# A state-space layer's output gathered for two chunks at a time: one TensorE burst and one PSUM bank in place of two

## The chip, the cores and the metric

The kernel runs on one core of one Trainium2 chip. The metric is the device time of one execution in microseconds; several runs are made and their median is taken. One execution is recorded by the hardware profiler. The engines are TensorE (PE, with its weight loads shown apart as PEld), VectorE (DVE), ScalarE (ACT), GpSimd (POOL) and SyncE (SP), which here only issues DMAs. Each engine takes its own instructions strictly in the order in which they stand in the program; engines wait for each other through semaphores.

## What is computed

The reference is an encoder of two layers over 1024 tokens of width 1024. Layer 0 is attention and is not touched. Layer 1 is a bidirectional state-space (Mamba-2 SSD) layer, with 32 heads in 8 groups of 4, 128 states and chunks of 128 tokens. Cut to what matters (one direction):

```
xbc = silu(conv(h @ w_in))            # x, B, C; z and dt come from the same product
cb = einsum('bclgn,bcsgn->bcgls', cc, bc)
y_diag = einsum('bcgrls,bclgrp...', cb * decay, x * dt)
states = einsum('bclgn,bclgrp->bcgrpn', bc, x * dt * decay_states)
carry = carry * chunk_decay + states  # over the chunks, one after the other
y_off = einsum('bclgn,bcgrpn->bclgrp', cc, carry_before) * exp(acs)
y = (y_diag + y_off of both directions + x * d_skip) * silu(z)
```

After it come an RMS norm, the product with `w_out`, a gate, a residual and a last norm. Everything is float32; the large products are made exact enough by splitting each operand into a rounded high part and a low rest (three matmuls for one).

## The kernel before, in words

**Two streams in one.** The SSD work of a group of heads is too small to fill TensorE, so it is laid between the large matmuls of the projection `w_in` for the next group. `group_dense(g)` gives the dense stream: six blocks per group, in the order x0, z0, x1, B, C, z1. One block has 48 matmuls of 128x512 (L359 to L361, "dense" from here on) and fills two of the four PSUM banks named `acc`; the block after the next takes the same two banks again. A block of x0, x1, B or C is read from its banks eight times by VectorE, the taps of the convolution (L1336, in the rows `big<-acc,cv,big`), after ScalarE has put the middle tap into SBUF (L1328). The weights are loaded by SP, rounded by ScalarE (`whi`, L254), and the rest is made by VectorE (`wlo`, L255).

`ssd_items(g)` gives the other stream: a list of items, each with the time that it is thought to take on PE and DVE. `balance` lays the two streams into one order by these numbers. So a changed number or a merged item moves dense matmuls and SSD items against each other on all engines.

**The items of a group**, with the lines that the text speaks of:

- `A1(c)` turns x and B of chunk c by PE transposes (L1412). `A2(j)` scales x (`xd`, L1424), makes the chunk's states on PE (L1425) and adds the decayed carry: a product into a tile `sw` (L1434) and a sum into the new carry `SS` (L1435).
- `B0(c)` loads the summed decays of chunk c into a tile `acs` (one DMA of 512 KB issued by SP).
- `B1(c)`, for c from 7 down to 0: VectorE makes `E` (L1449, four instructions), PE the product of B and C (L1452), VectorE masks it into `cb` (L1455), ScalarE takes exponentials (`E`, L1457), copies `cb` times dt into `W` (L1459) and exponentials of `acs` (L1461).
- `M(c)`: VectorE adds the other direction to `W` (L1471, four), multiplies `E` by `W` (L1473) and `acs` by C (L1476).
- `B2(c)`: PE gathers y of chunk c in one bank (L1487; 12 matmuls with 64 columns of weights, 8 for the first and last chunk; the trace has two records for each), VectorE adds the skip term into `yt` (L1491, two of 128x128), GpSimd multiplies z by it (L1495, two of 128x128). It comes after `M` of the chunk below, right behind the product of `B1(c-2)`.

The y banks are `a2` and `a3` in turn. The buffers: `sw` 1, `acs` 4, `E` 3, `W` 2, `yt` 2 (128x256 each).

In group 7 the dense stream is the first part of the output product (L1004 to L1006), which asks of VectorE one scaled rest (L1584) and one `wlo` for every 12 matmuls.

Of the kernel before, what the change touches and what calls it, by code (L numbers as in the profile page):

```python
# [11 lines left out]
F32 = mybir.dt.float32  # L12
# [3 lines left out]
OP = mybir.AluOpType  # L16

P = 128
# [73 lines left out]
class Trunk:  # L92
# [1302 lines left out]
    def ssd_items(self, g):  # L1395
        nc = self.nc
        st = self.grp[g]
        ident = self.c("ident")
        C = 8
        hs = slice(4 * g, 4 * g + 4)  # L1400
        xt, bt, SS, live = {}, {}, {}, {}

        def ck(c):
            return slice(P * c, P * c + P)

        def coef(t, c):
            return t[:, c].rearrange("p (d h) -> p d h", d=2)[:, :, hs, None].to_broadcast([P, 2, 4, 64])

        def A1(c):
            p = self.bank("a0", [P, 3, P], 2)  # L1410
            for i, n in enumerate(("x0", "x1", "B")):
                nc.tensor.transpose(p[:, i], st[n][:, ck(c)], ident)  # L1412
            x = xt[c] = self.u("xt", [P, 4, 64], F32, 8)
            nc.scalar.copy(x.rearrange("p h q -> p (h q)"), p[:, :2].rearrange("p i q -> p (i q)"))
            b = bt[c] = self.u("bt", [P, P], F32, 8)
            nc.scalar.copy(b, p[:, 2])

        def A2(j):

            if j < C - 1:  # L1420
                p = live["s", j] = self.bank("a3" if j % 2 else "a2", [P, 2, 4, 64])
                for d, c in enumerate((j, C - 1 - j)):
                    xd = self.u("xd", [P, 4, 64], F32, 3)
                    nc.vector.tensor_mul(xd, xt[c], coef(self.dtdec, c)[:, d])  # L1424
                    nc.tensor.matmul(p[:, d].rearrange("p h q -> p (h q)"), bt[c], xd.rearrange("p h q -> p (h q)"),  # L1425
                                     start=True, stop=True)
            if j:
                p = live.pop(("s", j - 1))
                s = SS[j - 1] = self.u("SS", [P, 2, 4, 64], F32, 7)
                if j == 1:  # L1430
                    nc.scalar.copy(s, p)
                else:
                    w = self.u("sw", [P, 2, 4, 64])
                    nc.vector.tensor_mul(w, SS[j - 2], coef(self.cdec, j - 1))  # L1434
                    nc.vector.tensor_add(s, p, w)  # L1435

        def B0(c):
            a = live["a", c] = self.u("acs", [P, 2, 4, P], F32, 4)
            nc.sync.dma_start(a, self.acsd[c, :, hs][None].to_broadcast([P, 2, 4, P]))

        def dirs(c):

            return [d for d, k in ((0, c > 0), (1, c < C - 1)) if k]

        def B1(c):
            a = live["a", c]
            E, W = live["G", c] = self.u("E", [P, 4, P], F32, 3), self.u("W", [P, 4, P], F32, 2)
            for h in range(4):
                nc.vector.scalar_tensor_tensor(E[:, h], a[:, 0, h], self.delta[:, c, 4 * g + h:4 * g + h + 1], a[:, 1, h],  # L1449
                                               op0=OP.add, op1=OP.min)  # L1450
            p = self.bank("a0", [P, P], 2)
            nc.tensor.matmul(p, st["B"][:, ck(c)], st["C"][:, ck(c)], start=True, stop=True)  # L1452
            cb = live["cb", c] = self.u("cb", [P, 2, P])
            tri = self.cst[:, CST["upper"][0]:CST["lower"][1]].rearrange("p (d l) -> p d l", d=2)
            nc.vector.tensor_mul(cb, p[:, None].to_broadcast([P, 2, P]), tri)  # L1455
            for h in range(4):
                nc.scalar.activation(E[:, h], E[:, h], AF.Exp, bias=self.nacb[:, c, 4 * g + h:4 * g + h + 1])  # L1457
            for h in range(4):
                nc.scalar.activation(W[:, h], cb[:, 0], AF.Copy, scale=self.dt[:, c, 4 * g + h:4 * g + h + 1])  # L1459
            ds = slice(dirs(c)[0], dirs(c)[-1] + 1)  # L1460
            nc.scalar.activation(a[:, ds], a[:, ds], AF.Exp)  # L1461
            if c == 0 and g < 7:
                nc.scalar.preload_act_table_set(SILU)

        def M(c):

            cb = live.pop(("cb", c))
            E, W = live["G", c]
            for h in range(4):
                hh = 32 + 4 * g + h  # L1470
                nc.vector.scalar_tensor_tensor(W[:, h], cb[:, 1], self.dt[:, c, hh:hh + 1], W[:, h],  # L1471
                                               op0=OP.mult, op1=OP.add)
            nc.vector.tensor_mul(E, E, W)  # L1473
            ds = dirs(c)
            a = live["a", c][:, ds[0]:ds[-1] + 1].rearrange("p d h l -> p (d h) l")
            nc.vector.tensor_mul(a, a, st["C"][:, None, ck(c)].to_broadcast([P, 4 * len(ds), P]))  # L1476

        def B2(c):

            y = self.bank("a3" if c % 2 else "a2", [P, 2, P])  # L1480
            G, _ = live.pop(("G", c))
            ea = live.pop(("a", c))
            for r in range(2):
                mms = [(SS[6 - c if d else c - 1][:, d], ea[:, d]) for d in dirs(c)] + [(xt[c], G)]
                for k, (w, m) in enumerate(mms):
                    for i in range(2):
                        nc.tensor.matmul(y[64 * i:64 * i + 64, r], w[:, 2 * r + i], m[:, 2 * r + i],  # L1487
                                         start=k == 0, stop=k == len(mms) - 1)
            t = self.u("yt", [P, 2, P], F32, 2)
            for r in range(2):  # L1490
                nc.vector.scalar_tensor_tensor(t[:, r], st[f"x{r}"][:, ck(c)], self.sv[:, 2 * g + r:2 * g + r + 1],  # L1491
                                               y[:, r], op0=OP.mult, op1=OP.add)
            for r in range(2):
                z = st[f"z{r}"][:, ck(c)]
                nc.gpsimd.tensor_mul(z, z, t[:, r])  # L1495
            if c == 0 and g == 7:
                self.ylast = [st["z0"], st["z1"]]
            elif c == 0:
                for r in range(2):
                    nc.gpsimd.dma_start(self.yd[2 * g + r], st[f"z{r}"])  # L1500

        def a1(c):
            return 200, lambda: A1(c), 0.35, 0.8

        def a2(j):
            return 900, lambda: A2(j), 0.9, 2.3

        items = []
        for j in range(C // 2):
            items += [a1(j), a1(C - 1 - j)]  # L1510
            if j:
                items.append(a2(j - 1))
        items.append((1, lambda: (B0(C - 1), B0(C - 2)), 0, 0))
        items += [a2(j) for j in range(C // 2 - 1, C)]
        if g == 7:
            items.append((1500, lambda: None, 0, 2.0))
        for c in range(C - 1, -1, -1):
            items.append((900, lambda c=c: B1(c), 0.25, 1.6))
            if c < C - 2:
                items.append((500, lambda c=c: B2(c + 2), 1.7, 0.6))  # L1520
            items.append((1150, lambda c=c: M(c), 0, 3.0))
            if c > 1:
                items.append((1, lambda c=c: B0(c - 2), 0, 0))
        items += [(500, lambda: B2(1), 1.7, 0.6), (900, lambda: None, 0, 1.5), (500, lambda: B2(0), 1.7, 0.6)]
        return items

    def out1(self, tail):
# [301 lines left out]
```

## Time and profile before

| | us |
|---|---|
| median of 3 runs | 1833.21 (1831.17 to 1834.16) |
| the profiled execution, its device time | 1831.87 |
| its span in the trace | 1830.0 |
| SSD stages of groups 0 to 6, from the trace | about 988 to 1590 |
| SSD stage of group 7 | about 1590 to 1671 |

The profile's page gives PE busy for 97% of the span, DVE for 76%, ACT for 53% and POOL for 15%. In the 40 slices of the page DVE stands at 9 tenths through the SSD stages, at 6 or 7 before them. To read it: the share of the span tells which engine could be the limit, and the waits inside one stage tell whether it is. The trace of groups 1 to 6 repeats almost to the hundredth of a microsecond, every 89.3 us, so one group stands for six.

### The profile page before, as it was taken

To read this page: it belongs to the slowest core of one execution; us is meant where nothing else is said; L and a number is where in the kernel's file an instruction comes from. 1 tells how busy PE (TensorE), PEld (TensorE's weight loads), DVE (VectorE), ACT (ScalarE), POOL (GpSimd) and SP (SyncE) were. 2 spreads that over 40 slices of the span, in tenths; PEclk is the share of its full clock that TensorE was granted. 3 is DMA by queue.
4 is the path that set the end of the run, shared out by engine and by line. 5 is a ranking of instruction groups with operands and counts; after the bars stand their busy time and mean duration, and the time that the engine had idled before them with its cause. 6 is when DMAs were issued, how large, how long until landed. Compare 5 with 4: busy or idle time off the path is not lost.

```text
span 1830.0 us, 28629 instructions
## 1 busy us (share of the span) xinstructions
PE 1778.0 (97%) x10136; PEld 1463.5 (80%) x10136; DVE 1395.2 (76%) x3212; ACT 961.9 (53%) x2107; POOL 283.2 (15%) x466
## 2 busy tenths in 40 slices
PE   8999999999999999999999999999999999997997
PEld 6888888878788888789878788888888888776787
DVE  7576667767654664666687989899898989898965
ACT  6655444544454554444444656565656565765532
POOL 3102122112211221010010101010101010114310
PEclk8999999999999999999999999999999999999999
DMA  8132234323311221264213242333333232354542
GB/s 323 55 118 88 94 100 132 96 88 99 90 58 47 79 66 45 78 218 152 82 50 95 71 118 83 111 89 97 97 89 104 82 110 76 116 162 128 190 163 97
DMA packets 99734, 193.66 MB, mean 106 GB/s; under 512 B 15624, under 2 KB 23048, under 8 KB 99592
## 3 DMA queue, kind: packets, MB, share of 16 engines
q1 hardware_dynamic: 86600, 167.32, 29.7%
q0 software_dynamic: 12288, 23.86, 4.7%
q8 instruction: 80, 1.31, 0.3%
q10 hardware_dynamic: 704, 0.66, 0.1%
q14 instruction: 62, 0.51, 0.1%
HBM read 169.00 MB, written 16.48 MB: 101 GB/s over the span
## 4 chain that ended last, share of the span: by engine, by line
PE 83%; DVE 10%; ACT 4%; issue 2%; DMA 1%; SPq 0%; ACTq 0%; DVEq 0%; POOL 0%
PE acc L359 17%; PE acc L361 16%; PE acc L360 16%; PE a L1487 4%; PE a L1425 3%; PE a L1004 3%; PE a L1005 3%; PE a L1006 3%; PE acc L1006 2%; PE a L702 2%; PE acc L1004 2%; PE acc L1005 2%; PE a L687 2%; DVE big L1336 1%; DVE wlo L255 1%
## 5 line engine op out<-in xcount | busy, mean ns | idle before, releaser
L359 PE MATMUL acc<-big,whi 128*128 128x512 f32 (+1 forms) x1520 | 628.0, 413 | 0.8 <-DVE big L1336 0.7
L361 PE MATMUL acc<-big,wlo 128*128 128x512 f32 (+1 forms) x1520 | 593.8, 391 | 0.0
L360 PE MATMUL acc<-big,whi 128*128 128x512 f32 (+1 forms) x1520 | 592.7, 390 | 0.6 <-DVE big L277 0.6
L359 PEld LDWEIGHTS acc<-big,whi 128*128 128x128 f32 x1520 | 287.1, 189 | 66.0 <-issue 15.5
L361 PEld LDWEIGHTS acc<-big,wlo 128*128 128x128 f32 x1520 | 286.4, 188 | 63.1
L360 PEld LDWEIGHTS acc<-big,whi 128*128 128x128 f32 x1520 | 287.8, 189 | 48.4 <-DVE big L277 1.2
L255 DVE TENSOR_TENSOR wlo<-wraw,whi 128x512 fp32r<-128x512 f32 (+1 forms) x297 | 213.5, 724 | 79.8 <-ACT whi L254 76.8
L254 ACT CAST whi<-wraw 128x512 fp32r<-128x512 f32 (+1 forms) x302 | 181.9, 612 | 88.8 <-issue 26.6
L678 ACT ACTIVATE sm<-sm,nb 128x256 f32<-128x256 f32 (+1 forms) x192 | 89.3, 466 | 194.3 <-DVE nb L676 191.6
L1336 DVE SCALAR_TENSOR_TENSOR big<-acc,cv,big 128x512 f32<-128x512 f32 (+1 forms) x248 | 169.3, 741 | 6.5 <-ACT big L1328 6.5
L1495 POOL TENSOR_TENSOR big<-big,yt 128x128 f32<-128x128 f32 x128 | 61.6, 502 | 633.7 <-DVE yt L1491 633.7
L1457 ACT ACTIVATE E<-E,nacb 128x128 f32<-128x128 f32 x256 | 81.8, 391 | 128.7 <-DVE E L1449 113.3
L689 DVE COPY pt<-a 128x512 f32<-128x512 f32 (+1 forms) x96 | 57.6, 600 | 72.8 <-PE a L687 72.8
L673 DVE CUSTOM_DVE_ANT_0 sm<-a,cst 128x256 f32<-128x256 f32 (+1 forms) x192 | 64.9, 375 | 57.7 <-PE a L668 57.4
L1004 PE MATMUL a<-big,whi 128*128 128x256 f32 (+1 forms) x304 | 99.2, 326 | 0.0
L1006 PE MATMUL a<-big,wlo 128*128 128x256 f32 (+1 forms) x304 | 98.0, 323 | 0.7 <-DVE wlo L255 0.7
L1005 PE MATMUL a<-big,whi 128*128 128x256 f32 (+1 forms) x304 | 97.9, 322 | 0.0
L1328 ACT ACTIVATE big<-acc,cv 128x512 f32<-128x512 f32 x62 | 44.5, 770 | 95.2 <-PE acc L361 82.8
L1004 PE MATMUL acc<-big,whi 128*128 128x512 f32 x224 | 91.2, 407 | 2.6 <-ACT big L1348 2.6
L575 POOL DMA_DIRECT2D rt<-kT x92 | 50.3, 559 | 280.3 <-ACT kT L515 185.3
L1005 PE MATMUL acc<-big,whi 128*128 128x512 f32 x224 | 88.4, 395 | 3.1 <-DVE big L255 2.7
L1471 DVE SCALAR_TENSOR_TENSOR W<-cb,dt,W 128x128 f32<-128x128 f32 x256 | 85.1, 388 | 8.1 <-ACT W L1459 6.1
(257 smaller groups left out, 3147.6 us busy)
## 6 DMA issues: line engine op xcount, KB each, us to landing
wraw<-in_win SPq DMA_DIRECT2D x186, 256.0 KB
acs<-acsd SPq DMA_DIRECT2D x64, 512.0 KB
wraw<-in_wout SPq DMA_DIRECT2D x112, 256.0 KB
big<-in_modw SPq DMA_DIRECT2D x48, 512.0 KB
yd<-big POOLq DMA_DIRECT2D x14, 512.0 KB, 4.8
big<-yd SPq DMA_DIRECT2D x28, 256.0 KB
vT<-mix POOLq DMA_DIRECT2D x20, 256.0 KB, 4.9
big<-in_xT SPq DMA_DIRECT2D x8, 512.0 KB
```

Source lines behind the costliest of these rows:

```text
L254: self.nc.scalar.copy(dst_hi, src)
L255: self.late.append((lambda: self.lo_engine.tensor_sub(dst_lo, src, dst_hi.bitcast(F32)), tile))
L359: mm(o, hi[:, cols], x_[:, t0:t0 + n], start=first, stop=False, **kw)
L360: mm(o, hi[:, cols], x_[:, H2 + t0:H2 + t0 + n], start=False, stop=False, **kw)
L361: mm(o, lo[:, cols], x_[:, t0:t0 + n], start=False, stop=last, **kw)
L678: nc.scalar.activation(sm[:, h, :W], sm[:, h, :W], AF.Exp, bias=nb[:, h:h + 1], scale=0.125, accum_out=stat[:, h, 1, i:i + 1])
L1004: mm(o, hi[:, c], x[:, t:t + n], start=kt == 0 and (n == H2 or m % 2 == 0), stop=False, **kw)
L1005: mm(o, hi[:, c], x[:, H2 + t:H2 + t + n], start=False, stop=False, **kw)
L1006: mm(o, lo[:, c], x[:, t:t + n], start=False, stop=kt == nkt - 1, **kw)
L1336: nc.vector.scalar_tensor_tensor(y[:, lo:hi], a[:, lo + o:hi + o], w[:, cv, k:k + 1], y[:, lo:hi], op0=OP.mult, op1=OP.add)
L1457: nc.scalar.activation(E[:, h], E[:, h], AF.Exp, bias=self.nacb[:, c, 4 * g + h:4 * g + h + 1])
L1471: nc.vector.scalar_tensor_tensor(W[:, h], cb[:, 1], self.dt[:, c, hh:hh + 1], W[:, h], op0=OP.mult, op1=OP.add)
```

## The change

The items `B2(c)` of two chunks become one, `B2(c0)` for c0 = 6, 4, 2, 0: the matmuls of chunk c0+1 and then of c0 go into one bank (`a3` for 6 and 2, `a2` for 4 and 0), then two instructions of 128x256 on VectorE and two of 128x256 on GpSimd. The item comes after `B1(c0-2)`; the last two chunks come together at the end. The number of thought times for an item becomes 3.2 and 0.85 (it was 1.7 and 0.6 for one chunk). The decayed carry is made in the tile of the new carry, so `sw` goes. The buffers: `acs` 5, `E` 4, `W` 1, `yt` 1 (128x512). In the changed file the lines after L1434 stand one lower or one higher; the rows of order below have its numbers.

```diff
-                    w = self.u("sw", [P, 2, 4, 64])
-                    nc.vector.tensor_mul(w, SS[j - 2], coef(self.cdec, j - 1))
-                    nc.vector.tensor_add(s, p, w)
+                    nc.vector.tensor_mul(s, SS[j - 2], coef(self.cdec, j - 1))
+                    nc.vector.tensor_add(s, p, s)
...
-            a = live["a", c] = self.u("acs", [P, 2, 4, P], F32, 4)
+            a = live["a", c] = self.u("acs", [P, 2, 4, P], F32, 5)
...
-            E, W = live["G", c] = self.u("E", [P, 4, P], F32, 3), self.u("W", [P, 4, P], F32, 2)
+            E, W = live["G", c] = self.u("E", [P, 4, P], F32, 4), self.u("W", [P, 4, P])
...
-        def B2(c):
+        def B2(c0):
-            y = self.bank("a3" if c % 2 else "a2", [P, 2, P])
-            G, _ = live.pop(("G", c))
-            ea = live.pop(("a", c))
+            y = self.bank("a3" if c0 % 4 else "a2", [P, 2, 2, P])
+            for c in (c0 + 1, c0):
+                G, _ = live.pop(("G", c))
+                ea = live.pop(("a", c))
...
-            t = self.u("yt", [P, 2, P], F32, 2)
+            two = slice(P * c0, P * c0 + 2 * P)
+            t = self.u("yt", [P, 2, 2 * P])
             for r in range(2):
-                nc.vector.scalar_tensor_tensor(t[:, r], st[f"x{r}"][:, ck(c)], self.sv[:, 2 * g + r:2 * g + r + 1],
-                                               y[:, r], op0=OP.mult, op1=OP.add)
+                nc.vector.scalar_tensor_tensor(t[:, r], st[f"x{r}"][:, two], self.sv[:, 2 * g + r:2 * g + r + 1],
+                                               y[:, r].rearrange("p c l -> p (c l)"), op0=OP.mult, op1=OP.add)
...
-            if c < C - 2:
-                items.append((500, lambda c=c: B2(c + 2), 1.7, 0.6))
+            if c < C - 2 and c % 2 == 0:
+                items.append((500, lambda c=c: B2(c + 2), 3.2, 0.85))
...
-        items += [(500, lambda: B2(1), 1.7, 0.6), (900, lambda: None, 0, 1.5), (500, lambda: B2(0), 1.7, 0.6)]
+        items += [(900, lambda: None, 0, 1.5), (500, lambda: B2(0), 3.2, 0.85)]
```

What this does to the order is shown at two places of a group that stands for groups 1 to 6. The first is PE, where the dense block of z1 begins (its first matmul writes the bank that the block of B had). L1452 or L1451 is the product of chunk 0, L1487 the gathering of y. Before:

```order
L361 MATMUL acc_11857<-big_8756,wlo_11785 128x512
L1452 MATMUL a_2167_11980<-big_11049,big_10925 128x128
L1487 MATMUL a_2169_11994<-acs_11693,SS_11315 64x128 x2
L1487 MATMUL a_2169_11994<-acs_11693,SS_11371 64x128 x2
L1487 MATMUL a_2169_11994<-E_11804,xt_11252 64x128 x2
L1487 MATMUL a_2169_11994<-acs_11693,SS_11315 64x128 x2
L1487 MATMUL a_2169_11994<-acs_11693,SS_11371 64x128 x2
L1487 MATMUL a_2169_11994<-E_11804,xt_11252 64x128 x2
L359 MATMUL acc_12012<-big_8051,whi_11868 128x512
```

In the change:

```order
L361 MATMUL acc_11779<-big_8756,wlo_11689 128x512
L359 MATMUL acc_11878<-big_8051,whi_11790 128x512
L360 MATMUL acc_11878<-big_8051,whi_11790 128x512
L361 MATMUL acc_11878<-big_8051,wlo_11791 128x512
L359 MATMUL acc_11879<-big_8704,whi_11790 128x512
L360 MATMUL acc_11879<-big_8704,whi_11790 128x512
L361 MATMUL acc_11879<-big_8704,wlo_11791 128x512
L1451 MATMUL a_2129_11892<-big_10977,big_10826 128x128
L1487 MATMUL a_2131_11906<-acs_11559,SS_11282 64x128 x2
```

The block of z1 (acc_12012, now acc_11878) now begins ahead of chunk 0's product and ahead of the burst of chunks 3 and 2; before, the bursts of both lay in front of it. Over the whole group the order of PE before, with D for dense matmuls, P for the product and Y for matmuls of y, is P D42 P D24 P Y8 D12 P Y12 D18 P Y12 D36 P Y12 D18 P Y12 D36 P Y12 D6 Y12 D18 Y8; now it is P D48 P D18 P D24 P Y20 D6 P D42 P Y24 D12 P D42 P Y24 D18 Y20. The block of z1 begins with the 187th dense matmul in both.

The second place is VectorE at the first bursts of y (big is x there, a_2113, a_2123 and a_2088 are y's banks). Before, chunks 7 and 6:

```order
L1449 SCALAR_TENSOR_TENSOR E_11576<-acs_11515,delta_8985 128x128 x4
L1455 TENSOR_TENSOR cb_11584<-a_2111_11582,cst_71 128x256
L1491 SCALAR_TENSOR_TENSOR yt_11604<-big_10488,sv_8811,a_2113_11595 128x128
L1491 SCALAR_TENSOR_TENSOR yt_11604<-big_10768,sv_8811,a_2113_11595 128x128
L1471 SCALAR_TENSOR_TENSOR W_11577<-cb_11584,dt_8982,W_11577 128x128 x4
L1473 TENSOR_TENSOR E_11576<-E_11576,W_11577 128x512
L1476 TENSOR_TENSOR acs_11515<-acs_11515,big_11049 128x1024
L1449 SCALAR_TENSOR_TENSOR E_11634<-acs_11574,delta_8985 128x128 x4
L1455 TENSOR_TENSOR cb_11642<-a_2121_11640,cst_71 128x256
L1491 SCALAR_TENSOR_TENSOR yt_11666<-big_10488,sv_8811,a_2123_11653 128x128
L1491 SCALAR_TENSOR_TENSOR yt_11666<-big_10768,sv_8811,a_2123_11653 128x128
L255 TENSOR_TENSOR wlo_11622<-wraw_11449,whi_11621 128x512
```

In the change, chunks 7 and 6 in one:

```order
L255 TENSOR_TENSOR wlo_11536<-wraw_11383,whi_11535 128x512
L1448 SCALAR_TENSOR_TENSOR E_11570<-acs_11508,delta_8985 128x128 x4
L1454 TENSOR_TENSOR cb_11578<-a_2086_11576,cst_71 128x256
L1492 SCALAR_TENSOR_TENSOR yt_11610<-big_10453,sv_8811,a_2088_11589 128x256
L1492 SCALAR_TENSOR_TENSOR yt_11610<-big_10675,sv_8811,a_2088_11589 128x256
L1470 SCALAR_TENSOR_TENSOR W_11571<-cb_11578,dt_8982,W_11571 128x128 x4
L1472 TENSOR_TENSOR E_11570<-E_11570,W_11571 128x512
L1475 TENSOR_TENSOR acs_11508<-acs_11508,big_10977 128x1024
L1448 SCALAR_TENSOR_TENSOR E_11631<-acs_11559,delta_8985 128x128 x4
L1454 TENSOR_TENSOR cb_11639<-a_2095_11637,cst_71 128x256
L1336 SCALAR_TENSOR_TENSOR big_11567<-acc_11451,cv_8809,big_11567 128x512
```

The first `yt` now stands one chunk later, behind `cb` of chunk 4 instead of chunk 5, is twice as wide, and waits for the last matmul of both chunks; in chunk 3 the taps of x1 (the last row and the seven after it, with one `wlo` among them) now follow `cb` directly. Over the whole program VectorE has 64 instructions fewer, PE as many as before.

## Rows read from the trace of the kernel before

**Rows 1.** Page, the chain that ended last, share of the span by engine:

```profile
PE 83%; DVE 10%; ACT 4%; issue 2%; DMA 1%; SPq 0%; ACTq 0%; DVEq 0%; POOL 0%
```

**Rows 2.** Windows: stretch, us, busy (count) of PE, PEld, DVE, ACT, POOL, PEclk, DMA:

```profile
1162.55:1251.82 89.27, 88.97 (x533) 73.23 (x532) 80.58 (x174) 52.29 (x121) 8.77 (x18) 1.00 0.34 95
...
1618.70:1670.58 51.88, 40.14 (x302) 33.16 (x300) 50.05 (x115) 37.75 (x93) 9.43 (x16) 0.97 0.48 134
```

**Rows 3.** Waits of PE: 1000 to 1590, then 1600 to 1680; total, times, longest:

```profile
PE a L1487 <- DVE acs L1476: 1.9, 1, 1.9
...
PE a L1487 <- DVE acs L1476: 9.9, 4, 4.9
```

**Rows 4.** Chain in order of time, 1100 to 1140: start, us, what (records):

```profile
1109.41 1.46 PE a L1487 x24
1110.87 0.43 PE acc L359
...
1111.76 0.23 PE acc L359
...
1134.31 1.02 PE a L1487 x16
```

**Rows 5.** Timeline of PE: product of chunk 5, first matmul of block z1:

```profile
1178.06 0.38 PE L1452 MATMUL a<-big,big 128*128 128x128 f32 x2
...
1216.17 0.50 PE L359 MATMUL acc<-big,whi 128*128 128x512 f32 x1
```

**Rows 6.** Timeline of DVE, last taps of B:

```profile
1211.36 2.71 DVE L1336 SCALAR_TENSOR_TENSOR big<-acc,cv,big 128x511 f32<-128x511 f32 x4
```

**Rows 7.** Timeline of DVE, one chunk from E on, and taps of x1:

```profile
1189.34 1.13 DVE L1449 SCALAR_TENSOR_TENSOR E<-acs,delta 128x128 f32<-128x128 f32 x4
1190.39 0.41 DVE L1455 TENSOR_TENSOR cb<-a,cst 128x256 f32<-128x256 f32 x1
1190.72 0.59 DVE L1491 SCALAR_TENSOR_TENSOR yt<-big,sv,a 128x128 f32<-128x128 f32 x2
1191.39 1.36 DVE L1471 SCALAR_TENSOR_TENSOR W<-cb,dt,W 128x128 f32<-128x128 f32 x4
1192.78 0.69 DVE L1473 TENSOR_TENSOR E<-E,W 128x512 f32<-128x512 f32 x1
1193.39 1.22 DVE L1476 TENSOR_TENSOR acs<-acs,big 128x1024 f32<-128x1024 f32 x1
1194.53 2.72 DVE L1336 SCALAR_TENSOR_TENSOR big<-acc,cv,big 128x512 f32<-128x512 f32 x4
1197.16 0.68 DVE L255 TENSOR_TENSOR wlo<-wraw,whi 128x512 fp32r<-128x512 f32 x1
1197.76 2.72 DVE L1336 SCALAR_TENSOR_TENSOR big<-acc,cv,big 128x511 f32<-128x511 f32 x4
```

**Rows 8.** Timeline of DVE in chunk 7, where no POOL instruction runs:

```profile
1169.77 1.14 DVE L1471 SCALAR_TENSOR_TENSOR W<-cb,dt,W 128x128 f32<-128x128 f32 x4
1170.94 0.69 DVE L1473 TENSOR_TENSOR E<-E,W 128x512 f32<-128x512 f32 x1
```

**Rows 9.** Timelines of DVE and of POOL in group 7:

```profile
1633.17 3.47 DVE L1471 SCALAR_TENSOR_TENSOR W<-cb,dt,W 128x128 f32<-128x128 f32 x4
...
1633.88 2.63 POOL L1556 TENSOR_TENSOR big<-big,big 128x512 f32<-128x512 f32 x2
1641.49 0.93 POOL L1495 TENSOR_TENSOR big<-big,yt 128x128 f32<-128x128 f32 x2 [4.99 <-DVE yt L1491]
```

**Rows 10.** Timeline of ACT, the casts behind chunk 3's exponentials:

```profile
1193.09 1.12 ACT L254 CAST whi<-wraw 128x512 fp32r<-128x512 f32 x2
```

**Rows 11.** Timeline of PE: two instructions and the idle time ahead of each:

```profile
1597.37 0.79 PE L1004 MATMUL acc<-big,whi 128*128 128x512 f32 x1 [2.58 <-ACT big L1348]
...
1651.92 0.66 PE L1487 MATMUL a<-acs,SS 128*64 128x128 f32 x8 [2.12 <-DVE acs L1476]
```

**Rows 12.** Windows right behind those two idle times:

```profile
1597.37:1602.72 5.35, 5.35 (x16) 4.38 (x17) 5.03 (x9) 4.50 (x10) 0.80 (x1) 0.50 0.03 11
1651.92:1656.00 4.08, 4.08 (x35) 3.45 (x36) 3.99 (x12) 2.58 (x9) 0.93 (x2) 1.00 0.40 126
```

More of the change, by code (lines that the diff above doesn't have):

```diff
@@ L1476, in M @@
             nc.vector.tensor_mul(a, a, st["C"][:, None, ck(c)].to_broadcast([P, 4 * len(ds), P]))
-        def B2(c):
-            y = self.bank("a3" if c % 2 else "a2", [P, 2, P])
-            G, _ = live.pop(("G", c))
-            ea = live.pop(("a", c))
-            for r in range(2):
[L1484 to L1488, printed above, removed]
-            t = self.u("yt", [P, 2, P], F32, 2)
+        def B2(c0):
[3 more added lines that the diff above has]
+                ea = live.pop(("a", c))
+                for r in range(2):
+                    mms = [(SS[6 - c if d else c - 1][:, d], ea[:, d]) for d in dirs(c)] + [(xt[c], G)]
+                    for k, (w, m) in enumerate(mms):
+                        for i in range(2):
+                            nc.tensor.matmul(y[64 * i:64 * i + 64, r, c - c0], w[:, 2 * r + i], m[:, 2 * r + i],
+                                             start=k == 0, stop=k == len(mms) - 1)
+            two = slice(P * c0, P * c0 + 2 * P)
+            t = self.u("yt", [P, 2, 2 * P])
+            for r in range(2):
+                nc.vector.scalar_tensor_tensor(t[:, r], st[f"x{r}"][:, two], self.sv[:, 2 * g + r:2 * g + r + 1],
+                                               y[:, r].rearrange("p c l -> p (c l)"), op0=OP.mult, op1=OP.add)
             for r in range(2):
-                nc.vector.scalar_tensor_tensor(t[:, r], st[f"x{r}"][:, ck(c)], self.sv[:, 2 * g + r:2 * g + r + 1],
-                                               y[:, r], op0=OP.mult, op1=OP.add)
-            for r in range(2):
-                z = st[f"z{r}"][:, ck(c)]
+                z = st[f"z{r}"][:, two]
                 nc.gpsimd.tensor_mul(z, z, t[:, r])
-            if c == 0 and g == 7:
+            if c0 == 0 and g == 7:
                 self.ylast = [st["z0"], st["z1"]]
-            elif c == 0:
+            elif c0 == 0:
                 for r in range(2):
```

## The prediction, as it was made before the changed kernel had run

> **What bounds the kernel now.** I read the chain that ended last first: PE holds 83% of it and DVE 10% [rows 1]. Then the windows by stage. In one SSD group of 89.27 us PE is busy for 88.97 and DVE for 80.58 [rows 2]; groups 1 to 6 are alike, so PE is the limit there and DVE has 8.7 us to spare. In group 7 the roles change: in 51.88 us PE is busy for 40.14 and DVE for 50.05 [rows 2]. The waits say the same: PE waits for DVE's product on `acs` once, for 1.9 us, up to 1590, and for 9.9 us in group 7 [rows 3].
>
> **What the merged bursts save on PE.** A burst of y has a fixed price. 24 records take 1.46 us and 16 take 1.02, so one record costs 0.055 and entering the burst 0.14; the first dense matmul behind it takes 0.43 instead of 0.23 [rows 4]. That is 0.14 + 0.20 = 0.34 us per burst beside its records. A group has eight bursts and will have four, with the same records: 4 x 0.34 = 1.36 us per group. If nothing else happened, seven groups would give 9.5 us; in group 7 PE waits for DVE anyway.
>
> **What the new order puts in the way.** By the order in the section on the change, the dense block of z1 begins with the 187th dense matmul and takes the banks of the block of B. It must wait until VectorE has finished B's taps on them. Before, the last four taps start at 1211.36; the third of them frees the first bank, at 1211.36 + 2 x 0.66 + 0.74 = 1213.4 [rows 6]. PE comes at 1216.17 [rows 5]: 2.75 us to spare, and no wait.
>
> *When PE comes now.* Between the product of chunk 5 (1178.06) and the block lie 120 dense matmuls in both kernels. Before, six bursts with 136 records lie there too (6 x 0.34 + 136 x 0.055 = 9.5 us), now two with 88 (5.5 us); the product of chunk 0, an estimated 0.2 us from its two records, also falls behind the block. So PE comes 4.2 us earlier, at 1212.0.
>
> *When the bank is free now.* VectorE cannot take `yt` of chunks 7 and 6 before the 40 records of both have run. The burst starts behind 24 dense matmuls of 0.23 and two products: 1178.06 + 0.2 + 5.5 + 0.3 = 1184.1, and ends 0.14 + 40 x 0.055 + 0.1 later, at 1186.5. From there VectorE has no gap until B's taps, and I add its instructions from start to start [rows 7]: E 1.05, cb 0.33, taps 2.63 for four, `wlo` 0.60, E times W 0.61, `acs` 1.14; W takes 1.17 for four where POOL is quiet [rows 8].
>
> The wide `yt` is the new part. A narrow one starts 0.26 after the one ahead and a 512 wide tap 0.66 (between the two, 256 columns: 0.39). From `yt` to E times W took 2.06 [rows 7]. W is what stretches: beside two POOL instructions of 1.31 us four W take 3.47 instead of 1.14 [rows 9], two of them one POOL instruction each. So W waits for GpSimd instruction by instruction. POOL's product takes 0.46 for 128 columns and its sum 1.31 for 512 [rows 9], so 0.74 for 256, 0.28 more each. From the wide `yt` to E times W I take 2.06 + 2 x 0.28 + 0.13 for the later start = 2.75.
>
> The Trainium skill, "SBUF — State Buffer", section "SBUF: two separate sides", states it as a lock: DVE instructions with two SBUF inputs and GpSimd instructions exclude each other for a whole instruction. By that rule, the trace agrees (3.47 against 1.14). If the two only shared bandwidth, 2.06 would hardly grow, each of the two wide `yt` below would be 0.7 cheaper, and the wait worked out next would be about 1.3 us, which cancels PE's gain.
>
> One more wait is new: in chunk 3 `wlo` now comes right behind `cb` and four taps, 4.0 us after E; ScalarE casts its `whi` 3.75 us after E (1193.09 against 1189.34) for 0.6 us [rows 7, 10]. That is 0.4 us.
>
> The sum from 1186.5: chunk 4: 2.75 + 0.61 + 1.14 = 4.5. Chunk 3: 1.05 + 0.33 + 2.63 + 0.4 + 0.60 + 2.63 + 1.17 + 0.61 + 1.14 = 10.56. Chunk 2 with a `wlo` ahead and two taps behind: 0.60 + 1.05 + 0.33 + 2.75 + 0.61 + 1.14 + 1.32 = 7.8. Chunk 1 up to the third of the last four taps: 1.05 + 0.33 + 1.32 + 0.60 + 1.32 + 0.74 = 5.36. Together 28.2: the bank is free at 1214.7. PE comes at 1212.0 and **waits 2.7 us**. Everything behind it on PE waits with it: chunk 0's product, both last bursts, the next group's transposes. Per group: 2.7 - 1.36 = 1.35 us slower; for groups 1 to 6, **+8.1 us**.
>
> The wait has bounds. Without POOL's stretching and the cast's delay it is 0.9 (1.35 - 0.45 - 1.36 below nothing: a gain of 0.45 per group); with 0.6 us more on DVE it is 3.3 (+2.0 per group).
>
> **The clock.** An idle PE can lose its clock. After 2.58 us of idle [rows 11] the granted clock is 0.50, 1.2 GHz, for 5.35 us [rows 12]; after 2.12 us it stays 1.00. The new wait lies at the edge. Half a clock for 5.35 us costs 2.7; I count one and a half of the six groups: **+4.0** (between 0 and 16).
>
> **Group 0 and group 7.** In group 0 PE already waits 1.9 for DVE [rows 3]; either limit moves there, I take 0 (-1.4 to +1.4). In group 7 DVE sets the pace. Ahead of the last product three chunks lose their `yt` (2.06 becomes 1.17, three times 0.9) and three get a wide one (three times 0.7): **-0.6** (-3 to +2).
>
> **What costs nothing.** The carry made in its own tile keeps one product and one sum; the product now waits for the readers of that tile, y's bursts of the group before, which stand ahead on PE. One `W` instead of two: ScalarE's next W needs `cb`, which VectorE writes only after E times W, so the wait is there already. A fifth `acs` and a fourth `E` hold what the later burst holds longer; SP issues the load behind chunk 7's release about 2 us later but the tile is read some 15 us on. Without those buffers each load would wait for the merged burst. VectorE's 64 saved instructions (128 times 0.26 against 64 times 0.39, some 8 us) are no gain by themselves where it waits for PE's burst.
>
> **The sum**: 8.1 + 4.0 + 0 - 0.6 = +11.5 us on the profiled 1831.87, which lies 1.3 below the median of 1833.21. Against the median: 1844.7, said as 1844.
>
> **The rivals.**
>
> *VectorE's relief carries, faster.* The wait at z1's bank does not come, because DVE is sooner than my sum: it decides when the bank is free before 1212.0, 2.7 us sooner than I have it. Then PE's saving stands: 7 x 1.36 + 0.6 = 10 us, 1823. For it speaks that DVE has 8.7 us to spare per group [rows 2]; against it that no spare time lies between 1186.5 and the taps. The Trainium skill, "Perfetto Trace Analysis", section "Optimizing Scalar/DVE Operations", names a fixed overhead for each DVE instruction and advises fewer, larger ones; by that rule the change gains, and the narrow and wide starts (0.26, 0.66 for four times the width) agree with it. 17%.
>
> *The two cancel, no change.* The wait is near 1.4 us, as it would be if W were not held up: 1833. 15%.
>
> *The clock falls in every group, slower still.* 8.1 - 0.6 + 16 gives 1857. Against it: 2.12 us of idle did not do it. 8%.
>
> *My forecast*: slower by the bank's wait, with the clock falling once or twice; without any fall 1840.7. Its own range is 1837 to 1852. 60%.
>
> **How the numbers follow.** Some 0.2%, 3.7 us, is what a measurement of this kernel can tell from no change. Faster 0.17, same 0.15, slower 0.68. The range leaves out about 15% below, where the relief carries in full, and about 5% above: 1828 to 1856.
>
> **What would show it.** Right: a new row among PE's waits, dense L359 waiting for DVE's taps (L1336), 2 to 3 us once in each of groups 1 to 6; bursts of y of 2.3 and 2.8 us, four per group; `yt` waiting for PE at the first of them; W of 1.7 us and more behind a wide `yt`; the group's period at 90 to 92 us; stretches at clock 0.50 behind the wait. Wrong: no such wait and a period of 88 us (the relief), or the same wait with a period of 89.3 (they cancel), or a new wait elsewhere, of ScalarE or of the loads of `acs`.

## The result, and the profile after

The changed kernel takes 1855.76 us (median of four runs, 1854.79 to 1858.38) against 1833.68 for the kernel before (1831.17 to 1836.48): 22.1 us slower, a ratio of 1.0119 with a 95% interval of 1.0107 to 1.0131. The direction was forecast, the size was not: 1844.0 had been predicted, 10.8 us over the median before. The time lies where the rival "the clock falls in every group" had put it (1857).

The page of the changed kernel: its span, the busy time of the engines, and the shares of the chain that ended last.

```profile
span 1853.2 us, 28454 instructions
PE 1781.9 (96%) x10136; PEld 1471.0 (79%) x10136; DVE 1395.5 (75%) x3148; ACT 962.9 (52%) x2107; POOL 270.5 (15%) x402
PE 74%; DVE 17%; ACT 4%; issue 2%; DMA 2%; SPq 0%; ACTq 0%; DVEq 0%; POOL 0%
```

PE's share of the chain falls from 83% to 74% and DVE's grows from 10% to 17% [rows 1]. The waits of PE from 1126 to 1591 us, where groups 1 to 6 meet their block of z1 (who waits, for whom, total, times, longest):

```profile
PE acc L359 <- DVE big L1336: 16.9, 6, 2.9
PE a L1412 <- ACT bt L1416: 1.5, 5, 0.3
```

The first row is new. In the kernel before, from 1000 to 1590, PE waits for DVE's product on `acs` once [rows 3] and for `xd` twice, and never for taps:

```profile
PE a L1425 <- DVE xd L1424: 1.0, 2, 0.6
```

It is the wait that was forecast, at the place that was forecast, once in each of six groups. One of them on PE's timeline (start, duration, what, and in brackets the idle time before it and what ended it):

```profile
1216.67 0.39 PE L361 MATMUL acc<-big,wlo 128*128 128x512 f32 x1
1219.97 0.47 PE L359 MATMUL acc<-big,whi 128*128 128x512 f32 x1 [2.90 <-DVE big L1336]
...
1220.53 0.63 PE L361 MATMUL acc<-big,wlo 128*128 128x512 f32 x1
1220.95 0.63 PE L359 MATMUL acc<-big,whi 128*128 128x512 f32 x1
1221.38 0.63 PE L360 MATMUL acc<-big,whi 128*128 128x512 f32 x1
```

Without the wait the next matmul would start 0.23 behind 1216.67, at 1216.90; it starts at 1219.97, so 3.07 us are lost. Two matmuls later they start 0.43 apart instead of 0.23. The windows show why (stretch, its length, busy time and count of PE, PEld, DVE, ACT and POOL, PE's granted clock, DMA share, GB/s): a whole group, then the wait, then 3 us behind it, then the 3 us after those.

```profile
1167.38:1260.04 92.66, 89.45 (x533) 74.38 (x532) 80.86 (x166) 52.44 (x121) 7.04 (x10) 0.98 0.35 92
1216.90:1219.90 3.00, 0.16 (x1) 0.00 (x0) 3.00 (x6) 3.00 (x6) 0.00 (x0) 1.00 0.22 81
1220.50:1223.50 3.00, 3.00 (x15) 2.36 (x15) 2.97 (x7) 0.00 (x0) 0.00 (x0) 0.50 0.25 93
1224.00:1227.00 3.00, 3.00 (x44) 2.69 (x41) 2.11 (x7) 2.66 (x9) 0.18 (x1) 1.00 0.00 0
```

In this group the clock is 1.00 while PE stands still, 0.50 (1.2 GHz) when it works again, and 1.00 after that. Taken in slices of 0.5 us, the low stretch is 3.42 us long, the same in each of groups 1 to 5; in group 6 it is twice as long. The group, 89.27 long before [rows 2], now takes 92.66. VectorE has eight instructions fewer in it (166 for 174) and is not less busy: 80.86 for 80.58.

Where the 23.2 us of the two spans lie is read from the first product of a group (timelines of PE, of the kernel before and then of the changed one, at the start of groups 1 and 7):

```profile
1073.25 0.27 PE L1452 MATMUL a<-big,big 128*128 128x128 f32 x1
...
1618.70 0.27 PE L1452 MATMUL a<-big,big 128*128 128x128 f32 x1
```

```profile
1074.79 0.38 PE L1451 MATMUL a<-big,big 128*128 128x128 f32 x2
...
1640.29 0.38 PE L1451 MATMUL a<-big,big 128*128 128x128 f32 x2
```

The changed kernel is 1.54 us late at the start of group 1 (0.92 of it already at the start of group 0, and 0.86 of that ahead of the first changed instruction: the `xd` at 959.76 starts at 960.62) and 21.59 at the start of group 7. So six groups cost 20.05 us, 3.34 each. Group 7 gives 0.3 back (its last product on `acs` starts at 1689.98 instead of 1668.70), and 1.9 come behind it.

### The profile page after: what moved, and what is told of

It reads as the page before. It is cut to its first block, busy times and chain, and to the rows that moved or that the text cites. A ratio compares the mean times of both kernels' runs of the same rounds, so it can differ in the third digit from the quotient of the medians.

```text
span 1853.2 us, 28454 instructions
## 1 busy us (share of the span) xinstructions
PE 1781.9 (96%) x10136; PEld 1471.0 (79%) x10136; DVE 1395.5 (75%) x3148; ACT 962.9 (52%) x2107; POOL 270.5 (15%) x402
## 4 chain that ended last, share of the span: by engine, by line
PE 74%; DVE 17%; ACT 4%; issue 2%; DMA 2%; SPq 0%; ACTq 0%; DVEq 0%; POOL 0%
PE acc L359 15%; PE acc L360 15%; PE acc L361 15%; DVE big L1336 4%; PE a L1487 3%; PE a L1425 3%; PE a L1004 2%; PE a L1006 2%; PE a L1005 2%; PE a L702 2%; PE acc L1006 2%; DVE W L1470 2%; PE acc L1004 2%; DVE wlo L255 2%; PE acc L1005 2%
## 5 line engine op out<-in xcount | busy, mean ns | idle before, releaser
L1496 POOL TENSOR_TENSOR big<-big,yt 128x256 f32<-128x256 f32 x64 | 47.6, 764 | 662.2 <-DVE yt L1492 603.2
L1470 DVE SCALAR_TENSOR_TENSOR W<-cb,dt,W 128x128 f32<-128x128 f32 x256 | 93.7, 422 | 6.5 <-ACT W L1458 6.5
```

## Experiments

All ran beside the kernel before, whose median was 1834 to 1836 there. Ratios are to it.

### The clock alone: e1_filler

```diff
             if kt == 0:
+                if fill:
+                    f = self.bank("a0", [P, H2], 2)
+                    for _ in range(fill):
+                        self.nc.tensor.matmul(f, self.whl[b - 1][0][:, :P], self.hn[0][0][:, :H2], start=True, stop=True)
```

`fill` is 8 for the block of z1 in the projections for groups 1 to 7, which run beside the SSD items of groups 0 to 6, and 0 for all others.

> The changed kernel with eight matmuls of 512 columns, whose result nobody reads, put on PE ahead of the block of z1 in groups 1 to 7: they run in the time in which PE would wait for B's taps (8 x 0.227 = 1.8 us of 2.8) and do nothing else. Theory (PE's idle time of 2.8 us lowers the granted clock, and that costs about 1.85 us per group behind the wait): the wait shrinks to about 1.0 us with the same end, the granted clock stays 1.00, and the time falls by 6 x 1.85 = 11 us to about 1845. Rival (the clock's fall is a mark in the record and costs little, or it does not come from the idle time): the time stays at 1855 to 1858.

1846.22 us, ratio 1.0066 (1.0051 to 1.0081): 9.5 us under the changed kernel for 56 matmuls more. Waits of PE over two groups, and the windows of one group and of the stretch behind its wait:

```profile
PE acc L359 <- DVE big L1340: 2.1, 2, 1.1
```

```profile
1128.70:1219.70 91.00, 89.61 (x541) 74.42 (x540) 80.72 (x167) 52.27 (x121) 7.01 (x10) 1.00 0.33 93
1220.00:1224.00 4.00, 4.00 (x54) 3.66 (x54) 3.97 (x10) 0.00 (x0) 0.00 (x0) 1.00 0.18 66
```

The bank comes no sooner, PE only passes the time with work, and the clock stays at 1.00. Each group takes 91.0 instead of 92.5. So the fall of the clock cost about 1.5 us in each of six groups, some 9 of the 22 us, and it comes from the wait. The theory holds; its 11 us were a little too many.

### The bank: e2_taps and e7_order

```diff
-                        when = pos + 1, i
+                        when = pos + 1, 0 if m == 2 else i
```

> The changed kernel with all eight taps of B emitted behind the first step of the block of C, so that VectorE does them in one row, ahead of E and cb of chunk 1 and of one wlo (1.05 + 0.33 + 0.60 = 2.0 us). Theory (the whole loss hangs on the bank of B): the wait at z1 falls from 2.8 to about 0.9 us, the clock does not fall, and each of six groups gains 2.0 + 1.85: 1855.8 - 23 = about 1833, between 1829 and 1838. Rival (VectorE as a whole is too late, the bank is only the first place where it shows): the wait moves to the last bursts or to cb of chunk 1, and less than a third comes back, 1848 or more.

1847.59 us, ratio 1.0071 (1.0056 to 1.0086). A miss: 8 of the 22 us came back, not all. (The edit also puts one chunk's product some 24 matmuls later on PE.) The waits of PE in one group:

```profile
PE acc L359 <- DVE big L1336: 0.9, 1, 0.9
PE a L1425 <- DVE xd L1424: 0.5, 1, 0.5
PE acc L361 <- DVE wlo L255: 0.5, 1, 0.5
PE a L1487 <- DVE acs L1475: 0.4, 1, 0.4
```

The wait at the bank is the 0.9 us that were expected, but what had been put behind the taps is late now: a `wlo`, the product on `acs` for the last burst, and `xd` of the next group. All are VectorE's. The theory was changed after this run, and the next one tests the change by moving PE instead: the burst of chunks 3 and 2 is taken out of the items for groups 0 to 6 and hung on the last step of the block of C.

```diff
+            if m == 5 and g:
+                late.setdefault((4, KT - 1), []).append((500, lambda: self.early[g - 1](), 3.2, 0.85))
...
-            if c < C - 2 and c % 2 == 0:
+            if c in (2, 4) or c == 0 and g == 7:
                 items.append((500, lambda c=c: B2(c + 2), 3.2, 0.85))
```

> The changed kernel with one step moved on PE alone: in groups 0 to 6 the burst of chunks 3 and 2 is issued ahead of the block of z1 (and with it ahead of chunk 0's product), as the bursts of both chunks stood before the change; VectorE's order stays. Rival (the bank of z1 alone is the loss, by an unlucky order on PE): PE is busy with the burst while B's taps end, no wait is left, the whole 1.36 us per group are gained: 1825 to 1829. Theory, changed after the run with the taps in one row (VectorE's chain from the first merged burst to chunk 0's product on acs and to xd is what is late; the bank is only where PE meets it first): PE then waits about 2.2 us in the last burst for chunk 0's acs (ready 1229.4, PE there 1227.1 in the times of the changed kernel's second group) and some 0.8 for xd; the period is about 91.1 instead of 92.5 and the time about 1847, 1843 to 1851.

1848.19 us, ratio 1.0075 (1.0060 to 1.0090); the theory had 1847, the rival 1825 to 1829. The waits of PE over two groups:

```profile
PE a L1489 <- DVE acs L1477: 4.2, 2, 2.2
PE a L1427 <- DVE xd L1426: 1.1, 2, 0.6
```

No wait for taps is left, and PE waits 2.1 us for chunk 0's `acs` and 0.55 for `xd` instead. The bank was only where PE met a late VectorE first. The periods say the same: where the clock does not fall, a group takes 91.0 to 91.3 us in e1_filler, in e2_taps and in groups 1 and 2 of e7_order alike. Moving the taps or the burst gave back no more than the clock's share.

### What makes VectorE late: e3_late, e9_ahead, e4_parts

`B2` is parted: its matmuls stay, and `B3` with `yt` and the product on GpSimd is called later.

```diff
+            if c == 3:
+                items.append((1, lambda: B3(6), 0, 0))
...
+            if c == 0:
+                items.append((1, lambda: B3(2), 0, 0))
             items.append((1150, lambda c=c: M(c), 0, 3.0))
+            if c == 2:
+                items.append((1, lambda: B3(4), 0, 0))
```

> The changed kernel with the wide yt (and the product on GpSimd behind it) of chunks 7 and 6 moved behind cb of chunk 3, and that of chunks 5 and 4 behind the product on acs of chunk 2, so that no W stands behind them and VectorE doesn't wait for the burst; bursts on PE as in the change. Theory (of the delay of the bank, 0.9 us is VectorE's wait for the merged burst and about 0.9 us each is W held up by GpSimd's product; part of it is ScalarE's W, which stays): the bank comes free about 1.4 us sooner, the wait is about 1.4 us and the clock stays: 6 x (1.4 + 1.85) = 19.5, so about 1836, between 1831 and 1845. Rival (GpSimd and the burst's end don't matter for the bank, VectorE's sum is the same): 1854 to 1858.

1837.58 us, ratio 1.0020 (1.0011 to 1.0030): 18 of the 22 us come back by moving four instructions of VectorE and four of GpSimd in each group; PE's order is unchanged. First the timelines of VectorE and GpSimd in the changed kernel, behind the first merged burst, then VectorE's in e3_late for the same chunk.

```profile
1190.11 0.42 DVE L1454 TENSOR_TENSOR cb<-a,cst 128x256 f32<-128x256 f32 x1
1191.43 0.87 DVE L1492 SCALAR_TENSOR_TENSOR yt<-big,sv,a 128x256 f32<-128x256 f32 x2 [0.91 <-PE a L1487]
1192.22 2.10 DVE L1470 SCALAR_TENSOR_TENSOR W<-cb,dt,W 128x128 f32<-128x128 f32 x4
1194.35 0.69 DVE L1472 TENSOR_TENSOR E<-E,W 128x512 f32<-128x512 f32 x1
...
1192.35 1.56 POOL L1496 TENSOR_TENSOR big<-big,yt 128x256 f32<-128x256 f32 x2 [47.19 <-DVE yt L1492]
```

```profile
1187.41 0.42 DVE L1454 TENSOR_TENSOR cb<-a,cst 128x256 f32<-128x256 f32 x1
1188.36 1.23 DVE L1470 SCALAR_TENSOR_TENSOR W<-cb,dt,W 128x128 f32<-128x128 f32 x4 [0.54 <-ACT W L1458]
1189.63 0.69 DVE L1472 TENSOR_TENSOR E<-E,W 128x512 f32<-128x512 f32 x1
```

In the changed kernel VectorE stands still for 0.91 us until the burst of both chunks ends, and then its four W take 2.10 while GpSimd's two products run beside them. One by one they take 0.35, 0.83, 0.83 and 0.34 us: the two that meet a GpSimd product (0.80 and 0.78 long) are the long ones, and ScalarE's W had ended 0.3 us before the first. With `yt` elsewhere the four take 1.23, and only ScalarE's W holds them up, for 0.54. From `cb` to E times W it is 4.24 us in the one and 2.22 in the other; 0.79 of the difference is `yt` itself, which only comes later, and the rest is gain (0.86 of it W, 0.37 less standing still). The wait at the bank is 1.2 us there, the clock stays at 1.00, and a group takes 89.45. By the exclusion of GpSimd and a VectorE instruction with two SBUF inputs that the prediction cited from the Trainium skill ("SBUF — State Buffer", section "SBUF: two separate sides") W had to be long beside GpSimd and short away from it; the runs agree (2.10 and 1.23). The taps, which read one of their inputs from a PSUM bank, are not held up: behind the moved `yt` they run beside the same two products and take 0.74 us each, as they do elsewhere.

e9_ahead moves the product on PE, in `B1(c)` of the changed kernel; `B1pe(c)` is its bank and its matmul.

```diff
+            if c == C - 1:
+                B1pe(c)
+            if c:
+                B1pe(c - 1)
```

> The changed kernel with each chunk's product (P) issued on PE one chunk sooner, so that cb no longer waits for PE (two waits of 0.8 us per group). Theory (the chain is anchored at the end of the first merged burst, for which VectorE waits 0.9 us with yt; what it wins ahead of that it loses in this wait): the wait for the burst grows by what cb's waits shrink, the bank comes free no sooner, and the time stays within 3 us of 1855. Rival (VectorE's delay builds up over the whole group): 1.6 us sooner at the bank, no clock fall, 1836 to 1840.

1851.56 us, ratio 1.0090 (1.0075 to 1.0105), half a microsecond outside what was expected. VectorE's waits in one group of the changed kernel, then of e9_ahead:

```profile
DVE yt L1492 <- PE a L1487: 1.8, 2, 0.9
DVE cb L1454 <- PE a L1451: 1.6, 2, 0.8
DVE W L1470 <- ACT W L1458: 1.0, 2, 0.5
```

```profile
DVE yt L1499 <- PE a L1494: 2.0, 2, 1.3
DVE W L1477 <- ACT W L1465: 1.7, 2, 1.2
DVE cb L1461 <- PE a L1446: 0.8, 1, 0.8
```

One of the two waits of `cb` is gone, and the wait of `yt` for the first burst grew from 0.9 to 1.3, that of W from 1.0 in all to 1.7. The group still takes 92.5 and PE still waits 2.5 us at z1. What the profiled execution gains, 2.2 us of span, lies between the starts of groups 6 and 7 (100.52 us for 102.95), where the low stretch of the clock is 3.4 us long instead of 6.8. So the chain that counts begins at the end of the first merged burst.

> The kernel before with the other parts of the change alone: five acs, four E, one W, and the decayed carry made in the new carry's tile; bursts, yt and their order as before. Theory: these cost nothing, 1833, within 3 us. Rival (one W, or the product that now waits for the readers of the carry's tile, is what makes VectorE late): 1840 or more.

1834.91 us, ratio 1.0001 (0.9991 to 1.0010), as expected: the carry in its own tile, one W and the other buffers cost nothing by themselves. All of the loss is in the merging.

### Whether the merging can pay: e6_early to e14_yt

e6_early is e3_late and e7_order in one.

> Both moves together: yt of chunks 7 to 4 later on VectorE (as in e3_late) and the burst of chunks 3 and 2 ahead of z1 on PE (as in e7_order). Theory (VectorE's chain is the bound, and in e3_late its xd is ready at about the time PE asks for it): the wait at the bank goes, about 1.0 us comes back in the last burst and in xd, the period stays at 89.2 to 89.5, and the time at 1835 to 1838. Rival (the bank was the last wait): period 88.1, time about 1829.

1838.96 us, ratio 1.0020 (1.0011 to 1.0030): 1 us over the expected range, with the expected period (89.45). PE's waits over three groups:

```profile
PE a L1427 <- DVE xd L1426: 1.6, 3, 0.5
PE a L1489 <- DVE acs L1477: 1.5, 3, 0.5
```

VectorE is still the later engine, by about 1 us per group. What then of the 8.7 us in which it idles per group in the kernel before? The waits of VectorE there, over one group:

```profile
DVE xd L1424 <- ACT xt L1414: 3.6, 1, 3.6
DVE xd L1424 <- PE a L1425: 1.3, 2, 1.1
DVE W L1471 <- ACT W L1459: 1.0, 1, 1.0
DVE cb L1455 <- PE a L1452: 0.9, 1, 0.9
```

These four make 6.8 of the 8.7 us. They are waits inside the chain (for the transposed x, for a product, for ScalarE's half of W), and in this order of the program VectorE cannot use them to catch up: in e6_early, where it is the late engine, all four are still there (3.6, 1.3, 2.1 and 1.6 us). Only another order removes some of them, as e10_cb shows below.

e8_ahead is e6_early with the products one chunk sooner (the edit of e9_ahead).

> e6_early with each chunk's product issued one chunk sooner on PE. Theory: here yt no longer anchors VectorE at the burst's end, so the two waits of cb (0.8 us each) are won by the whole chain, and PE's saving shows: period 88.0 to 88.5, time 1828 to 1832, faster than the kernel before by some 3 us. Rival (another wait, of W for ScalarE or of yt for the burst, takes all of it): 1835 to 1838.

1841.92 us, ratio 1.0039 (1.0026 to 1.0053), a miss: the rival was right and even too kind. VectorE's waits in one group:

```profile
DVE W L1479 <- ACT W L1467: 3.2, 4, 1.2
DVE cb L1463 <- PE a L1448: 0.8, 1, 0.8
```

W for ScalarE takes what `cb` gave, 3.2 us for 2.1 in e6_early: ScalarE makes its four exponentials of E before its four W, so an earlier `cb` alone doesn't help. e10_cb removes that; `CB(c)` is VectorE's masking that makes `cb`, taken out of `B1(c)`.

```diff
+            for h in range(4):
+                nc.scalar.activation(W[:, h], live["cb", c][:, 0], AF.Copy, scale=self.dt[:, c, 4 * g + h:4 * g + h + 1])
             for h in range(4):
                 nc.scalar.activation(E[:, h], E[:, h], AF.Exp, bias=self.nacb[:, c, 4 * g + h:4 * g + h + 1])
-            for h in range(4):
-                nc.scalar.activation(W[:, h], cb[:, 0], AF.Copy, scale=self.dt[:, c, 4 * g + h:4 * g + h + 1])
...
+            if c:
+                CB(c - 1)
             nc.vector.tensor_mul(E, E, W)
```

> e8_ahead with cb of a chunk made on VectorE one chunk sooner (behind the W of the chunk before it) and ScalarE's W put ahead of its exponents of E, so that VectorE's W waits for neither PE nor ScalarE (3.2 us for W and 0.8 for cb per group in e8_ahead). Theory (VectorE's chain sets the period of the changed kernel; its 8.7 us of idle time per group before were waits inside this chain, not spare time): the chain becomes some 3 to 4 us shorter, PE no longer waits in groups 1 to 6, and the merged bursts' saving shows: period 87.9 to 88.3 against 89.27 before, 1822 to 1829, faster than the kernel before. Rival (the merged bursts save nothing on PE in the end, or another wait follows at once): 1834 or more.

1830.60 us, ratio 0.9980 (0.9970 to 0.9989): faster than the kernel before, though 1.6 us short of what was expected, with 88.5 per group. e13_cb_before has these moves and the earlier product in the kernel before.

> The kernel before with the same two moves (products one chunk sooner on PE, cb one chunk sooner on VectorE, ScalarE's W ahead of its exponents), bursts and yt unmerged. Theory: in groups 1 to 6 PE has no wait that VectorE could lift, so the period stays at 89.27; group 7, where VectorE sets the pace, gains 2 to 5 us: 1829 to 1833. Rival (VectorE's relief shortens groups 1 to 6 too): 1826 or less.

1835.26 us, ratio 1.0002 (0.9993 to 1.0011), a group 89.26 long. Without the merged bursts VectorE's relief is worth nothing, as the theory says for groups 1 to 6; the gain in group 7 that was expected did not come.

> e10_cb with the burst of chunks 3 and 2 back at the change's place on PE, behind the beginning of the block of z1. Theory: with VectorE's chain 3 to 4 us shorter the bank of B is free when PE asks for it, so the place of this burst no longer matters and the time is that of e10_cb within 2 us. Rival (the order on PE is a cause of its own): a wait of 1 us or more stays at z1 in each group, 6 us over e10_cb.

1830.35 us, ratio 0.9973 (0.9963 to 0.9984), that of e10_cb: with VectorE's chain short enough, the place of the burst on PE no longer matters. A rest of it is left at z1, 0.2 us of idle PE per group. e14_yt takes the last overlap of W and GpSimd out of e10_cb:

```diff
-            items.append((1150, lambda c=c: M(c), 0, 3.0))
+            items.append((1150, lambda c=c: (M(c), B3(2)) if c == 0 else M(c), 0, 3.0))
```

> e10_cb with yt of chunks 3 and 2 behind the products of chunk 0, ahead of four taps, so that no W of VectorE stands beside GpSimd's product any more. Theory (in e10_cb VectorE's chain still lies some 0.6 us over PE's own 87.9 per group): the last 0.8 us of W held up by GpSimd leave the chain, acs of chunk 0 is ready when PE asks, period 87.9 to 88.1, some 3 us under e10_cb: 1826 to 1829. Rival (what is left in e10_cb is ScalarE's or PE's own): 88.5 and 1830 as before.

1823.64 us, ratio 0.9933 (0.9920 to 0.9947): 12 us faster than the kernel before and 32 faster than the change. One group of it, and all waits of PE in four groups:

```profile
1225.28:1313.19 87.91, 87.61 (x532) 73.04 (x532) 78.12 (x168) 52.77 (x121) 6.80 (x11) 1.00 0.35 97
```

```profile
PE a L1414 <- ACT bt L1418: 1.5, 5, 0.3
```

PE waits for VectorE nowhere in these groups, and the period is 87.91: 89.27 less 1.36, the saving of four bursts as it was predicted. The order of PE, ScalarE and GpSimd is that of e10_cb; the four W of chunk 0 take 1.14 us instead of 1.94 there. It came out better than expected (1826 to 1829) because it gained outside groups 1 to 6 too. Of the 6.4 us by which its span is shorter than that of e10_cb, 2.9 lie in those groups, 1.7 are there when group 1 begins (PE's wait for `acs` in group 0 is 1.1 us instead of 2.6), and 1.8 come behind the start of group 7.

## Why the prediction was wrong in size and right in kind

Each step by its own number, for a group:

- **PE's saving, 1.36.** Right. It is hidden in the changed kernel and stands free in e14_yt, where the period is 1.36 shorter; e13_cb_before, with the products and `cb` moved and the bursts apart, stays at 89.26.
- **PE comes sooner, the bank later; a wait of 2.7.** Right in place and cause, 3.07 in size. The group starts 4.83 us later than in the kernel before (1167.38 for 1162.55), so PE was forecast at 1216.8 and comes at 1216.9; the bank was forecast for 1219.5 and PE has it at 1219.97. Of the 0.4 missing, 0.17 lie between `yt` and E times W of chunk 4 (2.92 for 2.75); the stretches of chunks 3, 2 and 1 came out as summed (10.56, 7.81 and 5.35 for 10.56, 7.8 and 5.36). For six groups the wait less the saving is 10.3 us instead of 8.1.
- **The clock, "I count one and a half of the six groups: +4.0".** This is the step that failed. The rows showed a fall after 2.58 us of idle time and none after 2.12, and the predicted wait of 2.7 was above both; calling it the edge and counting one fall in four had nothing behind it. All six fell. One fall cost less than the 2.7 that were taken, since the stretch behind it was 3.42 us long (twice that in group 6) and not 5.35: half of it, 1.7, or 1.5 by e1_filler. The 5.35 was not the length of a low stretch either, but a window laid into one: in the kernel before PE works at 0.50 from 1597.37 to 1603.43, for 6.06 us. Six falls make 9 to 10 us, not 4.
- **Group 0, 0; group 7, -0.6.** 0.6 and -0.3, within their bounds. The 0.9 us ahead of the first group and the 1.9 behind the last were not foreseen, and their cause stays open; the first product of group 0 starts anywhere from 988.1 to 990.2 in the runs here.
- **What costs nothing.** Right for the carry and the buffers (e4_parts). The rival that VectorE's relief carries rested on its 8.7 us of idle time per group, and e6_early shows that most of these were waits of the chain itself.

The sum: 10.3 for the wait less the saving, 9 to 10 for the clock, some 3 for the rest: 22 to 23 us against 23.2 of the spans. What came true is the rival with a fall in every group, to which 8% were given. That its 1857 lies so near the measured 1855.76 is luck: it took 16 us for the clock, where 9 to 10 were lost, and 8.1 and -0.6 for the rest, where 10.3 and some 3 came.

The rule of the Trainium skill on fewer, larger VectorE instructions ("Perfetto Trace Analysis", section "Optimizing Scalar/DVE Operations") was taken to speak for a gain. The section says so of an engine that is saturated, and adds that where VectorE or ScalarE is not saturated but holds up other engines, breaking instructions up may let work end sooner. VectorE was busy for 80.58 of 89.27 us [rows 2], and the wide `yt` made it wait 0.91 us for both chunks: for the change as it was, the addition is the part that fits. By busy time the change shows no gain either, 80.86 us per group for 80.58: `yt` takes 3.5 us instead of 4.8, but W, beside GpSimd's wider products, takes 11.8 instead of 10.4. In e14_yt, where W stands beside none of them, `yt` takes the same 3.5 and W 9.2, and VectorE is busy for 78.12.

## What to carry to other kernels

When two results are gathered in one burst, the readers of the first wait for the end of the second, and whatever those readers set off next is late by as much; look at what follows them on the same engine before counting the saved overhead. Idle time of an engine is a reserve only if it lies outside the chain; of the 8.7 us per group here 6.8 were waits inside it. Put GpSimd's work beside instructions of VectorE that it does not hold up (here the taps). And a new wait of PE that is as long as one behind which the trace shows a fall of the clock is best counted with that fall each time, as all six showed it here, though the next section has a longer wait without one.

## What was not expected of the hardware

How long PE stood still did not alone decide whether its clock fell. In e7_order the same wait comes once in each group, 2.0 to 2.2 us long. The timeline of PE at two of them, and the windows behind:

```profile
1228.33 0.44 PE L1489 MATMUL a<-acs,SS 128*64 128x128 f32 x4 [2.16 <-DVE acs L1477]
...
1411.11 0.44 PE L1489 MATMUL a<-acs,SS 128*64 128x128 f32 x4 [2.04 <-DVE acs L1477]
```

```profile
1229.00:1232.00 3.00, 3.00 (x21) 2.38 (x18) 2.81 (x5) 2.68 (x6) 0.00 (x0) 1.00 0.00 0
1412.30:1415.30 3.00, 3.00 (x9) 2.34 (x10) 2.83 (x6) 1.53 (x3) 0.00 (x0) 0.50 0.00 0
```

The longer wait kept the clock at 1.00 (2.4 GHz) and the shorter one lost it; over the six groups it stayed in the first two and fell in the last four. In e6_early PE idles for 3.04 us in group 0 with no fall behind it. What else decides was not tried and stays open.
